# The fifth of seven products: one 512-column matmul for both parts of its operand, and two bank tags exchanged

## The chip, the cores and the metric

The kernel runs on one core of a Trainium2 chip. The metric is the device time of one execution in microseconds. The kernel before took 1758.14 us, the median of three runs (1758.01 to 1759.31).

The engines are named as the profile names them: PE is TensorE (PEld its weight loads), DVE is VectorE, ACT is ScalarE, POOL is GpSimd and SP is SyncE, which issues most transfers. PSUM is the memory that TensorE writes its products to. The program uses it in banks of 128 partitions by 512 float32 values.

## The reference

Two layers of a decoder trunk over 512 tokens of width 1024. In each layer: half a SwiGLU feed-forward, a mixer (a convolution, a sliding-window attention, an attention to a memory), a second half feed-forward, and a norm. Only the feed-forward is touched here:

```python
def swiglu(x, w1, w3, w2):
    return (jax.nn.silu(x @ w1) * (x @ w3)) @ w2

h = x + 0.5 * swiglu(rms_norm(x, ffn1_norm[l]), ffn1_w1[l], ffn1_w3[l], ffn1_w2[l])
...
h = h + 0.5 * swiglu(rms_norm(h, ffn2_norm[l]), ffn2_w1[l], ffn2_w3[l], ffn2_w2[l])
```

The inner width is 2816, that is 22 blocks of 128 columns. All of it is float32.

## The kernel before, in words

**Layout.** Activations are kept transposed: features on the partitions, the 512 tokens along a row. [...] ScalarE makes the high part (line 146) and VectorE subtracts it to get the low one (line 147). `whi` and `wlo` are the parts of a weight, `mh`/`ml` and `xhi`/`xlo` are buffers with the parts of the normed activations (`mh`, in spite of its name, holds high and low parts side by side, as do the three others).

**A feed-forward pass** (four in all) takes the 22 blocks in four quarters of 6, 6, 6 and 4. The first four blocks are done plainly. The other 18 are done in nine pairs, `f` = 4, 6, ... 20, by `up_pair`, and a quarter ends with the blocks' product with `w2` (lines 178 to 180 into the bank `mm`, and the addition to `h` in line 557). The blocks of a quarter's start are made ahead of that, so that pairs and `w2` work lie in each other's neighbourhood.

**A pair** multiplies the 1024 features by 256 columns, for `w1` and for `w3` (`i` = 0 and 1 in the loops), in 512 tokens. Features, columns and tokens are each halved, and the eight products of halves are replaced by seven, in the manner of Strassen and Winograd. Each of the seven has 512 features (4 blocks of 128, `k`), 128 columns and 256 tokens (`QT`). `M.m[j]` is the activations' operand of product number `j`: quarters and sums of quarters, made once in a pass. On the weights' side the sums are made for each pair: `X` is a sum of blocks, made by an ordinary transfer and one that adds (line 368, issued from POOL), in three buffers shared by all pairs, and `raw` gets two more sums by VectorE (line 398).

**Two ways to form a product.** `product` (line 379) uses twelve matmuls of 256 columns and adds all three kinds up in one half of a bank. `beside` (line 387) takes the operand's high and low parts, which lie next to each other, as one operand of 512 columns: four matmuls give high by high in a bank's first half and high by low in its second, and four of 256 columns add low by high to the first half. So it has eight matmuls, and its two halves must then be added, by VectorE.

**Banks.** There are eight: three with the tag `mm`, one `cf`, two `pt` and two `po`. A tag's banks are handed out in turn; a tile that asks for a tag waits until the tile that held that bank before has been read for the last time. The first pair of a pass (`f` = `PLAIN` = 4) uses `product` alone, with banks called `xy` and `zv`. The other eight pairs use banks called `x`, `y`, `c` and `v`. In them, products number 1, 6 and 5 are added up in `x` one after another, and ScalarE copies the sum out after each (lines 424 and 436 and their like); products 2, 3, 7 and 4 use `beside`. There are four passes of eight such pairs with two operands each.

**The order of the work.** The lines of the program say what depends on what. A scheduler in the framework makes one list of instructions for each engine from them, by its own simulated timeline. Each engine then takes its list strictly in order. A change of one product can so move instructions all over the pairs.

Of the kernel before, what the change touches and what calls it, by code (L numbers as in the profile page):

```python
# [13 lines left out]
AF = mybir.ActivationFunctionType  # L14
# [4 lines left out]
P = 128  # L19
D = 1024  # L20
S = 512
# [44 lines left out]
def trunk(ctx: ExitStack, tc: tile.TileContext, xT, memT, pos, w1a, w3a, w2a, w1b, w3b, w2b,  # L66
          wconv, wqk, wvm, wmem, wout, gains, small, rows, consts, out):
    nc = tc.nc
    V, G, A, T = nc.vector, nc.gpsimd, nc.scalar, nc.tensor
# [21 lines left out]
    def bank(shape, tag):  # L91

        if tag == "mm":
            return ps_mm.tile(shape, F32, tag=tag, name=tag)
        return ps_ax.tile(shape, F32, tag=tag, name=tag, bufs=1 if tag == "cf" else 2)

    def tm(name, tag="t", bufs=None):
        return tmp.tile([P, S], F32, tag=tag, name=name, **({"bufs": bufs} if bufs else {}))
# [4 lines left out]
    def raw_tile(src, cols):  # L103
        raw = wst.tile([P, UNIT], F32, tag="raw", name="raw", bufs=3)
        nc.sync.dma_start(raw[:, 0:cols], src)
        return raw
# [5 lines left out]
    first = []  # L112
# [72 lines left out]
    def blk(k, n=P):  # L185
        return slice(k * n, (k + 1) * n)
# [98 lines left out]
    QT = 256  # L285
# [65 lines left out]
    def gated():  # L351
        p = gated_pair()
        return [at(p, ALL, i, ALL) for i in range(2)]

    def unit(x):
        p = pair()
        split(p[0], p[1], x, V)
        return p

    def up_pair(l, w13, f, M):  # L360

        raw = [raw_tile(w13[i][l, f], D) for i in range(2)]
        X = []
        for i in range(2):

            x = wst.tile([P, UNIT], F32, tag="aux", name="wsum", bufs=3)
            nc.sync.dma_start(x.rearrange("p (f c) -> p f c", f=2), w13[i][l, f : f + 2, :, 0:QW].rearrange("f p c -> p f c"))
            G.dma_start(x, w13[i][l, f + 1], accum_op=ALU.add)
            X.append(x)
        z = wst.tile([P, UNIT], F32, tag="raw", name="raw", bufs=3)  # L370
        for i in range(2):
            nc.sync.dma_start(z[:, blk(i, QW)], w13[i][l, f + 1, :, QW:])
        x0, x1 = blk(0, QT), blk(1, QT)

        def product(ps, w, half, j, first=False):


            for n, (part, q) in enumerate([(0, q) for k in range(4) for q in ((k, 0), (k, 1))] + [(1, (k, 0)) for k in range(4)]):
                tail[0] = T.matmul(ps, w[part][:, blk(4 * half + q[0])], M.m[j][q[0]][:, q[1]], skip_group_check=True,  # L379
                                   start=first and not n, stop=n == 11)  # L380

        def beside(ps, w, half, j, first=False):


            def go(out, part, n):
                for k in range(4):
                    tail[0] = T.matmul(out, w[part][:, blk(4 * half + k)], M.m[j][k][:, 0:n], skip_group_check=True,  # L387
                                       start=first and not part and k == 0, stop=part == 1 and k == 3)

            go(ps, 0, 2)  # L390
            go(ps[:, 0], 1, 1)

        u, g = (tmp.tile([P, 2, S], F32, tag=t, name=t, bufs=n) for t, n in (("u", 1), ("g", 2)))
        part = [tm("part", "sq", 2) for _ in range(2)]
        to = (u, g)

        def add(out, a, b):
            V.tensor_tensor(out=out, in0=a, in1=b, op=ALU.add)

        def summed(out, ps, a):  # L400
            add(out, ps[:, 0], a)
            add(out, out, ps[:, 1])

        if f == PLAIN:
            xy = [bank([P, S], "po") for _ in range(2)]
            zv = [bank([P, S], "pt") for _ in range(2)]
            for i in range(2):
                w = unit(raw[i])
                product(xy[i][:, x0], w, 0, 1, first=True)
                product(xy[i][:, x1], w, 1, 2)  # L410
                A.activation(part[i], xy[i], AF.Copy)
                add(to[i][:, 0, x0], part[i][:, x0], part[i][:, x1])

                add(raw[i][:, 0:QW], raw[i][:, 0:QW], X[i][:, QW:])
                add(raw[i][:, QW:], raw[i][:, QW:], raw[i][:, 0:QW])
            for i in range(2):
                w = unit(raw[i])
                product(xy[i][:, x0], w, 0, 6)
                A.activation(part[i][:, x1], xy[i][:, x0], AF.Copy)
                product(zv[i][:, x0], w, 1, 3, first=True)  # L420
            for i in range(2):
                w = unit(X[i])
                product(xy[i][:, x0], w, 1, 5)
                A.activation(part[i][:, x0], xy[i][:, x0], AF.Copy)
                product(zv[i][:, x1], w, 0, 7)
                add(to[i][:, :, x1], zv[i].rearrange("p (n t) -> p n t", n=2), part[i][:, x0].unsqueeze(1).to_broadcast([P, 2, QT]))
            w = unit(z)
            for i in range(2):
                product(zv[i][:, x1], w, i, 4)
                add(to[i][:, 1, x0], zv[i][:, x1], part[i][:, x1])  # L430
        else:
            x = [bank([P, QT], "pt") for _ in range(2)]
            for i in range(2):
                w = unit(raw[i])
                product(x[i], w, 0, 1, first=True)
                A.activation(part[i][:, x0], x[i], AF.Copy)
                y = bank([P, 2, QT], "po")
                beside(y, w, 1, 2, first=True)
                summed(to[i][:, 0, x0], y, part[i][:, x0])

                add(raw[i][:, 0:QW], raw[i][:, 0:QW], X[i][:, QW:])
                add(raw[i][:, QW:], raw[i][:, QW:], raw[i][:, 0:QW])
            c, v = [bank([P, 2, QT], t) for t in ("cf", "mm")], []
            for i in range(2):
                w = unit(raw[i])
                product(x[i], w, 0, 6)
                A.activation(part[i][:, x1], x[i], AF.Copy)
                beside(c[i], w, 1, 3, first=True)
            for i in range(2):
                w = unit(X[i])  # L450
                v.append(bank([P, 2, QT], "po"))
                beside(v[i], w, 0, 7, first=True)
                A.activation(to[i][:, 1, x1], v[i][:, 0], AF.Copy)
                add(to[i][:, 1, x1], to[i][:, 1, x1], v[i][:, 1])
                product(x[i], w, 1, 5)
                A.activation(part[i][:, x0], x[i], AF.Copy)
                summed(to[i][:, 0, x1], c[i], part[i][:, x0])
                add(to[i][:, 1, x1], to[i][:, 1, x1], part[i][:, x0])
            w = unit(z)
            for i in range(2):  # L460
                beside(v[i], w, i, 4)
                summed(to[i][:, 1, x0], v[i], part[i][:, x1])
        out = gated()
        for n, sign in enumerate((1.0, -1.0)):
            A.activation(u[:, n], u[:, n], AF.Silu, scale=sign)
        M.gated = V.tensor_tensor(out=g, in0=g, in1=u, op=ALU.mult)
        for n, sign in enumerate((1.0, -1.0)):
            hi, lo = out[n]
            A.activation(hi, g[:, n], AF.Copy, scale=sign)
            V.scalar_tensor_tensor(out=lo, in0=g[:, n], scalar=sign, in1=hi.bitcast(F32), op0=ALU.mult, op1=ALU.subtract)  # L470
        return out

    def ffn(l, w13, w2, x, sums, factors, last, at_product, aside=None, closing=None):
# [55 lines left out]
        for q, (f0, nf) in enumerate(QUARTERS):  # L529
            ahead = 2 if q + 1 < len(QUARTERS) else 0  # L530
            for f in range(f0, f0 + nf + ahead, 2):
                if f not in g:
                    g[f], g[f + 1] = up_pair(l, w13, f, M)
                    if f == PLAIN:
                        with tc.issue_after(M.gated.ins):
                            rescale = after()
# [615 lines left out]
    for l in range(L):  # L1152
        x, new = nxt.x, Stat("st")
# [163 lines left out]
```

## Time and profile before

| what | us |
|---|---|
| median of three runs | 1758.14 |
| the profiled execution | 1758.82 |
| its span, first to last instruction | 1757.1 |
| TensorE busy | 1738.9 |
| VectorE busy | 1371.8 |
| ScalarE busy | 908.9 |

A row of the profile gives a line of the kernel, an engine, an operation, the tiles it writes and reads (`out<-in`) and their shapes. A busy time counts the time in which at least one instruction of a group ran. Matmuls overlap: a row says 0.39 us for one of 512 columns, while the next one starts after 0.23. For what a group costs, the start of the next group is therefore the measure, and not the sum of durations. An idle time in brackets is what an engine lost before an instruction, with what ended it.

### The profile page before, as it was taken

What the parts mean: (1) busy time and instruction counts of PE and PEld (TensorE: products, weight loads), DVE (VectorE), ACT (ScalarE), POOL (GpSimd) and SP (SyncE); (2) the same over time, 40 slices, a digit from 0 to 9 for tenths busy, and PEclk for the clock granted to TensorE, in tenths of its full rate; (3) what the DMA queues carried; (4) which work ended last, traced back from release to release, by engine and by line L of the source; (5) the groups of instructions that cost most, each with busy time, mean ns of one, the idle gap of its engine ahead of it and who ended that gap; (6) DMA issues with size and microseconds to landing.
All of it is one profiled execution on the core that took longest, in us unless ns stands there. A gap on an engine that the chain in (4) does not pass through costs nothing.

```text
span 1757.1 us, 26371 instructions
## 1 busy us (share of the span) xinstructions
PE 1738.9 (99%) x9980; PEld 1521.3 (87%) x9980; DVE 1371.8 (78%) x2218; ACT 908.9 (52%) x1437; POOL 196.5 (11%) x220
## 2 busy tenths in 40 slices
PE   8999999999999999999999999999999999999998
PEld 6889889888888989898889898988888889898987
DVE  6969878689877868687778787776898768686866
ACT  5546445356765535353655364544567655353533
POOL 1001000006221000000010010000251210000000
PEclk9999999999999999999999999999999999999999
DMA  9456645256348546465565565552661666464632
GB/s 272 121 173 162 174 132 156 78 159 155 96 87 190 131 136 171 139 166 146 146 155 158 154 169 156 156 144 68 167 160 57 136 152 177 132 174 128 156 99 85
DMA packets 97199, 253.49 MB, mean 144 GB/s; under 512 B 9904, under 2 KB 16304, under 8 KB 97072
## 3 DMA queue, kind: packets, MB, share of 16 engines
q1 hardware_dynamic: 78064, 190.45, 34.5%
q0 software_dynamic: 19008, 61.35, 19.4%
q8 instruction: 79, 1.29, 0.3%
q14 instruction: 48, 0.39, 0.1%
HBM read 249.67 MB, written 2.10 MB: 143 GB/s over the span
## 4 chain that ended last, share of the span: by engine, by line
PE 95%; DVE 2%; DMA 1%; issue 1%; ACT 0%; SPq 0%; DVEq 0%; POOLq 0%; ACTq 0%
PE pt L379 16%; PE mm L178 14%; PE mm L180 14%; PE mm L179 14%; PE po L387 14%; PE cf L387 2%; PE mm L387 2%; PE po L379 2%; PE po L178 2%; PE po L180 2%; PE po L179 2%; PE po L921 2%; PE mm L869 1%; DMA wsum<-in_w3a 1%; PE cf L178 1%; PE cf L179 1%
## 5 line engine op out<-in xcount | busy, mean ns | idle before, releaser
L146 ACT ACTIVATE whi<-raw 128x1024 fp32r<-128x1024 f32 (+3 forms) x346 | 326.1, 947 | 445.4 <-PE mm L179 218.6
L147 DVE TENSOR_TENSOR wlo<-raw,whi 128x1024 fp32r<-128x1024 f32 (+3 forms) x346 | 375.7, 1089 | 98.6 <-ACT whi L146 94.1
L179 PE MATMUL mm<-glo,whi 128*128 128x512 f32 (+1 forms) x752 | 292.2, 389 | 0.0
L178 PE MATMUL mm<-ghi,whi 128*128 128x512 f32 (+1 forms) x752 | 291.8, 390 | 0.0
L180 PE MATMUL mm<-ghi,wlo 128*128 128x512 f32 (+1 forms) x734 | 285.2, 389 | 0.0
L557 DVE SCALAR_TENSOR_TENSOR h<-mm,h 128x512 f32<-128x512 f32 x126 | 86.4, 689 | 117.2 <-PE mm L180 116.9
L178 PEld LDWEIGHTS mm<-ghi,whi 128*128 128x128 f32 x752 | 141.3, 188 | 29.2 <-DVE h L557 1.2
L179 PEld LDWEIGHTS mm<-glo,whi 128*128 128x128 f32 x752 | 141.3, 188 | 28.0
L180 PEld LDWEIGHTS mm<-ghi,wlo 128*128 128x128 f32 x734 | 137.9, 188 | 27.8
L387 PE MATMUL po<-xlo,whi 128*128 128x512 f32 x512 | 139.2, 393 | 0.0
L1051 DVE SCALAR_TENSOR_TENSOR there<-ypad,par,there 128x512 f32<-128x512 f32 x180 | 136.0, 779 | 1.5 <-issue 0.2
L178 PE MATMUL mm<-xhi,whi 128*128 128x512 f32 x272 | 108.6, 403 | 6.3 <-ACT xhi L156 6.3
L180 PE MATMUL mm<-xhi,wlo 128*128 128x512 f32 x272 | 107.1, 394 | 0.0
L179 PE MATMUL mm<-xlo,whi 128*128 128x512 f32 x272 | 107.0, 393 | 0.0
L387 PEld LDWEIGHTS po<-xlo,whi 128*128 128x128 f32 x512 | 89.6, 189 | 13.5
L147 DVE TENSOR_TENSOR wlo<-wsum,whi 128x1024 fp32r<-128x1024 f32 x72 | 87.6, 1217 | 0.6 <-ACT whi L146 0.4
L387 PEld LDWEIGHTS po<-xlo,wlo 128*128 128x128 f32 x512 | 78.3, 188 | 10.6
L146 ACT ACTIVATE whi<-wsum 128x1024 fp32r<-128x1024 f32 x72 | 76.2, 1059 | 20.3 <-PE po L387 16.4
L379 PE MATMUL pt<-xhi,whi 128*128 128x256 f32 x576 | 81.8, 283 | 0.0
L387 PE MATMUL po<-xlo,wlo 128*128 128x256 f32 x512 | 81.2, 280 | 0.0
L379 PEld LDWEIGHTS pt<-xhi,whi 128*128 128x128 f32 x576 | 74.9, 190 | 0.6
L379 PE MATMUL pt<-ml,whi 128*128 128x256 f32 x512 | 72.9, 282 | 0.0
(389 smaller groups left out, 3583.0 us busy)
## 6 DMA issues: line engine op xcount, KB each, us to landing
raw<-in_w2a SPq DMA_DIRECT2D x48, 384.0 KB, 3.5
raw<-in_w2b SPq DMA_DIRECT2D x48, 384.0 KB, 3.6
raw<-in_w1b SPq DMA_DIRECT2D x26, 512.0 KB, 3.5
raw<-in_w3b SPq DMA_DIRECT2D x26, 512.0 KB, 3.6
raw<-in_w1a SPq DMA_DIRECT2D x25, 512.0 KB, 3.5
raw<-in_w3a SPq DMA_DIRECT2D x25, 512.0 KB, 3.7
wsum<-in_w1a SPq DMA_DIRECT2D x18, 512.0 KB, 4.5
wsum<-in_w3a SPq DMA_DIRECT2D x18, 512.0 KB, 3.6
```

The lines of the kernel that those rows point to most:

```text
L146: a = A.activation(hi, x, AF.Copy)
L147: return a, on.tensor_tensor(out=lo, in0=x, in1=hi.bitcast(F32), op=ALU.subtract)
L178: T.matmul(ps, a[0], b[0], start=first, stop=False, **more)
L179: T.matmul(ps, a[0], b[1], start=False, stop=False, **more)
L180: tail[0] = T.matmul(ps, a[1], b[0], start=False, stop=last, **more)
L379: tail[0] = T.matmul(ps, w[part][:, blk(4 * half + q[0])], M.m[j][q[0]][:, q[1]], skip_group_check=True, start=first and not n, stop=n == 11)
L387: tail[0] = T.matmul(out, w[part][:, blk(4 * half + k)], M.m[j][k][:, 0:n], skip_group_check=True, start=first and not part and k == 0, st ...
L557: added = V.scalar_tensor_tensor(out=h[:, d, :], in0=ps, scalar=0.5, in1=h[:, d, :], op0=ALU.mult, op1=ALU.add)
L869: tail[0] = T.matmul(pp[i][:, z, :], q, k, start=not masked, stop=True, skip_group_check=True)
L921: tail[0] = T.matmul(po[:, 2 * c + i, :], ptb[:, i, j, :], v, start=(j == 0), stop=(j == nk - 1))
L1051: V.scalar_tensor_tensor(out=cv[:, c, :], in0=ypad[:, c, j : j + S], scalar=conv_w[:, c, j : j + 1], in1=cv[:, c, :], op0=ALU.mult, op1=AL ...
```

## The change

In the eight pairs after the first of each pass, product number 5 is formed with `beside` instead of `product`. Its bank `x` now has two halves. Products 1 and 6 use the first half alone, as before. Product 5 writes its high-by-low part to the second half, which nothing has written since the bank was begun, so it starts from nothing there. After ScalarE's copy of the first half into `part`, VectorE adds the second half to it.

In the first pair of each pass the tags of `xy` and `zv` are exchanged: `xy` takes `pt` and `zv` takes `po`. So the `x` of the next pair (tag `pt`) now follows on `xy`, and its `y` (tag `po`) on `zv`; before, it was the other way round.

```diff
         if f == PLAIN:
-            xy = [bank([P, S], "po") for _ in range(2)]
-            zv = [bank([P, S], "pt") for _ in range(2)]
+            xy = [bank([P, S], "pt") for _ in range(2)]
+            zv = [bank([P, S], "po") for _ in range(2)]
...
         else:
-            x = [bank([P, QT], "pt") for _ in range(2)]
+            x = [bank([P, 2, QT], "pt") for _ in range(2)]
             for i in range(2):
                 w = unit(raw[i])
-                product(x[i], w, 0, 1, first=True)
-                A.activation(part[i][:, x0], x[i], AF.Copy)
+                product(x[i][:, 0], w, 0, 1, first=True)
+                A.activation(part[i][:, x0], x[i][:, 0], AF.Copy)
                 y = bank([P, 2, QT], "po")
                 beside(y, w, 1, 2, first=True)
...
-                product(x[i], w, 0, 6)
-                A.activation(part[i][:, x1], x[i], AF.Copy)
+                product(x[i][:, 0], w, 0, 6)
+                A.activation(part[i][:, x1], x[i][:, 0], AF.Copy)
                 beside(c[i], w, 1, 3, first=True)
...
-                product(x[i], w, 1, 5)
-                A.activation(part[i][:, x0], x[i], AF.Copy)
+                beside(x[i], w, 1, 5)
+                A.activation(part[i][:, x0], x[i][:, 0], AF.Copy)
+                add(part[i][:, x0], part[i][:, x0], x[i][:, 1])
                 summed(to[i][:, 0, x1], c[i], part[i][:, x0])
                 add(to[i][:, 1, x1], to[i][:, 1, x1], part[i][:, x0])
```

The instruction lists of the two kernels, at three places. In the changed kernel, lines after 455 have a number one higher. First, TensorE in the first pass, at the end of pair `f` = 6: the fifth product of both operands (`pt`), product 4 or 7 (`po`) and the first matmuls of the product with `w2` (`mm`). Before:

```order
L379 MATMUL pt<-xhi,whi 128x256 x8
L379 MATMUL pt<-xhi,wlo 128x256 x4
L387 MATMUL po<-xlo,whi 128x512 x4
L387 MATMUL po<-xlo,wlo 128x256 x4
L178 MATMUL mm<-ghi,whi 128x512
L179 MATMUL mm<-glo,whi 128x512
L379 MATMUL pt<-xhi,whi 128x256 x8
```

And now:

```order
L387 MATMUL pt<-xhi,whi 128x512 x4
L387 MATMUL pt<-xhi,wlo 128x256 x4
L178 MATMUL mm<-ghi,whi 128x512
L179 MATMUL mm<-glo,whi 128x512
L387 MATMUL po<-xlo,whi 128x512 x4
L387 MATMUL po<-xlo,wlo 128x256 x4
L387 MATMUL pt<-xhi,whi 128x512 x4
```

The twelve matmuls of a fifth product have become eight, and two `w2` matmuls have moved ahead of the `po` product.

Second, TensorE in the first pass where the first pair (lines 379 alone) passes into pair `f` = 6, from the first operand's last `xy` product on. Before:

```order
L379 MATMUL po<-xhi,whi 128x256 x8
L379 MATMUL po<-xhi,wlo 128x256 x4
L379 MATMUL pt<-xlo,whi 128x256 x2
L387 MATMUL po<-mh,whi 128x512 x2
L387 MATMUL po<-ml,whi 128x512 x2
L379 MATMUL po<-xhi,whi 128x256 x8
L379 MATMUL po<-xhi,wlo 128x256 x4
L379 MATMUL pt<-xlo,whi 128x256 x7
```

And now:

```order
L379 MATMUL pt<-xhi,whi 128x256 x8
L379 MATMUL pt<-xhi,wlo 128x256 x4
L379 MATMUL po<-xlo,whi 128x256 x2
L379 MATMUL pt<-mh,whi 128x256 x8
L379 MATMUL pt<-xhi,whi 128x256 x8
L379 MATMUL pt<-xhi,wlo 128x256 x4
L379 MATMUL po<-xlo,whi 128x256 x7
```

The first work of pair 6 used to be its `y` (`po<-mh`, line 387) and is now its `x` (`pt<-mh`, line 379). Either way it follows the same two matmuls.

Third, VectorE in the first pass, near the end of pair `f` = 8, up to a split of the next weights (`wlo<-raw,whi`); `ypad` is a table that is made meanwhile. Before:

```order
L398 TENSOR_TENSOR u<-u,po 128x256
L601 TENSOR_TENSOR ypad<-ypad 128x128
L398 TENSOR_TENSOR u<-cf,part 128x256
L398 TENSOR_TENSOR g<-g,po 128x256
L698 TENSOR_TENSOR ypad<-ypad,gmem 128x256
L599 TENSOR_SCALAR ypad<-ypad 128x128
L398 TENSOR_TENSOR u<-u,cf 128x256
L580 SCALAR_TENSOR_TENSOR ypad<-ypad 128x128
L601 TENSOR_TENSOR ypad<-ypad 128x128
L147 TENSOR_TENSOR wlo<-raw,whi 128x1024
```

And now:

```order
L398 TENSOR_TENSOR u<-u,po 128x256
L602 TENSOR_TENSOR ypad<-ypad 128x128
L398 TENSOR_TENSOR part<-part,pt 128x256
L398 TENSOR_TENSOR g<-g,po 128x256
L699 TENSOR_TENSOR ypad<-ypad,gmem 128x256
L398 TENSOR_TENSOR part<-part,pt 128x256
L600 TENSOR_SCALAR ypad<-ypad 128x128
L398 TENSOR_TENSOR u<-cf,part 128x256
L581 SCALAR_TENSOR_TENSOR ypad<-ypad 128x128
L398 TENSOR_TENSOR u<-u,cf 128x256
L602 TENSOR_TENSOR ypad<-ypad 128x128
L147 TENSOR_TENSOR wlo<-raw,whi 128x1024
```

The two new additions (`part<-part,pt`) stand ahead of the split. The lists of the mixer, outside the feed-forward passes, are the same in both kernels, but for numbers.

## The prediction

> **What bounds the kernel now.** I read the page's first and fourth parts, then TensorE's waits, then its timeline in a calm stretch, then VectorE's share stage by stage. The busy line and the chain that ended last:
>
> ```profile
> PE 1738.9 (99%) x9980; PEld 1521.3 (87%) x9980; DVE 1371.8 (78%) x2218; ACT 908.9 (52%) x1437; POOL 196.5 (11%) x220
> PE 95%; DVE 2%; DMA 1%; issue 1%; ACT 0%; SPq 0%; DVEq 0%; POOLq 0%; ACTq 0%
> ```
>
> TensorE is the bound: 99% busy, 95% of the chain. A microsecond taken off its stream is a microsecond off the span, unless another engine cannot follow. The view of waits, TensorE alone, says how much idleness is left to win:
>
> ```profile
> PE mm L178 <- ACT xhi L156: 6.3, 2, 6.1
> ...
> PE po L387 <- ACT part L424: 0.7, 1, 0.7
> PE cf L387 <- ACT whi L146: 0.7, 2, 0.5
> PE po L387 <- DVE wlo L147: 0.6, 1, 0.6
> PE po L387 <- DVE u L398: 0.5, 1, 0.5
> PE pt L379 <- DVE g L398: 0.4, 1, 0.4
> ```
>
> The 6.3 us is the start of the program. The other five rows, 2.9 us together, all belong to the first two or three pairs of a feed-forward pass, and they are all that better order could give back there.
>
> **The change: TensorE's part.** Before and after, a fifth product streams 12 x 256 = 3072 columns; `beside` streams 4 x 512 + 4 x 256, also 3072. So no arithmetic is saved, only four instructions out of twelve. What four instructions are worth is read from TensorE's timeline of a pair in which it never waits; the columns are start, duration, operation and count, and the start of the next group ends the one before:
>
> ```profile
> 241.82 1.11 PE L379 MATMUL pt<-ml,whi 128*128 128x256 f32 x8
> ...
> 243.25 1.09 PE L387 MATMUL cf<-xhi,whi 128*128 128x512 f32 x4
> ...
> 244.65 1.11 PE L379 MATMUL pt<-ml,whi 128*128 128x256 f32 x8
> ...
> 246.08 1.09 PE L387 MATMUL mm<-xhi,whi 128*128 128x512 f32 x4
> ...
> 247.49 1.09 PE L387 MATMUL po<-xlo,whi 128*128 128x512 f32 x4
> ```
>
> A product of twelve takes 243.25 - 241.82 = 1.43 us, and 246.08 - 244.65 = 1.43 again; one of eight takes 244.65 - 243.25 = 1.40 and 247.49 - 246.08 = 1.41. The gain is 0.02 to 0.03 us each; I take 0.03 and, since the rows are rounded, allow 0.02 to 0.04. How many there are is the count of the ScalarE copies that follow a fifth product:
>
> ```profile
> L456 ACT ACTIVATE part<-pt 128x256 f32<-128x256 f32 x64 | 24.0, 375 | 14.2 <-PE pt L379 13.4 <-ACT u L453 0.8
> ```
>
> 64 x 0.03 = 1.9 us saved (bounds 1.3 and 2.6).
>
> [...]
>
> **VectorE's part.** Each of the 64 products now leaves its two parts in two halves of a bank, so VectorE gains 64 additions of 128x256, one operand from a bank. Its nearest rows are the other additions of line 398 that take 256 columns; the group and two neighbours in the timeline:
>
> ```profile
> L398 DVE TENSOR_TENSOR g<-g,part 128x256 f32<-128x256 f32 x32 | 13.3, 417 | 0.2
> ```
>
> ```profile
> 163.55 0.42 DVE L398 TENSOR_TENSOR g<-g,part 128x256 f32<-128x256 f32 x1
> 163.88 0.41 DVE L398 TENSOR_TENSOR g<-g,mm 128x256 f32<-128x256 f32 x1
> ```
>
> One lasts 0.42 us and the next starts after 0.33, so each new addition takes 0.33 us of the queue: 64 x 0.33 = 21 us of VectorE work, two (0.67 us) to a pair. ScalarE's copy of the first half stays as it was. Whether it counts depends on the stretch. By stage, the columns being length, then busy time and count of PE, PEld, DVE, ACT, POOL:
>
> ```profile
> 55.00:93.00 38.00, 36.68 (x276) 34.63 (x276) 36.73 (x51) 24.67 (x37) 3.02 (x4) 1.00 0.59 148
> 140.00:200.00 60.00, 59.32 (x401) 54.46 (x401) 58.31 (x125) 36.12 (x63) 8.62 (x8) 1.00 0.64 162
> 328.00:360.00 32.00, 32.00 (x190) 28.22 (x190) 20.91 (x36) 16.42 (x29) 0.11 (x1) 1.00 0.24 66
> 924.00:965.00 41.00, 40.45 (x306) 38.49 (x305) 35.65 (x50) 24.51 (x36) 3.46 (x4) 1.00 0.60 158
> 1012.00:1062.00 50.00, 49.53 (x343) 45.89 (x342) 45.05 (x77) 31.46 (x50) 5.95 (x6) 1.00 0.66 174
> 1446.00:1480.00 34.00, 34.00 (x266) 33.09 (x265) 32.15 (x43) 22.57 (x33) 2.59 (x3) 1.00 0.54 149
> ```
>
> In 328 to 360, a lone pair, VectorE is idle for 11 of 32 us; there 0.67 us is covered by that idleness (and would cost up to 0.67 us a pair without it). In the other five VectorE is 87 to 97% busy. The same windows, for the copies of line 456 alone, count the fifth products in them:
>
> ```profile
> 55.00:93.00 38.00, 0.39 (x1) 1.00 0.59 148
> 140.00:200.00 60.00, 1.95 (x6) 1.00 0.64 162
> 924.00:965.00 41.00, 0.37 (x1) 1.00 0.60 158
> 1012.00:1062.00 50.00, 1.52 (x4) 1.00 0.66 174
> 1446.00:1480.00 34.00, 0.37 (x1) 1.00 0.54 149
> ```
>
> Thirteen additions fall where VectorE is crowded: 13 x 0.33 = 4.3 us if every one reaches TensorE, nothing if none does. Most of that I do not charge, because TensorE hardly waits there as it is: 0.68 us in 140 to 200, and 0.47 in 1012 to 1062. What is behind the new addition in VectorE's queue matters at one point, the split of a pair's summed weights, whose end frees the buffer for the next sum's transfers. From the chain of waits and VectorE's timeline:
>
> ```profile
> 169.17 0.10 DVE wlo L147
> ...
> 170.43 4.52 DMA wsum<-in_w3a
> ...
> 175.50 6.52 DMA wsum<-in_w3a
> ...
> 184.69 1.20 PE cf L387 x4
> ```
>
> ```profile
> 157.26 1.23 DVE L147 TENSOR_TENSOR wlo<-raw,whi 128x1024 fp32r<-128x1024 f32 x1 [0.67 <-ACT whi L146]
> ```
>
> ```profile
> 1034.11 0.42 DVE L398 TENSOR_TENSOR g<-po,part 128x256 f32<-128x256 f32 x1 [1.42 <-PE po L387]
> ```
>
> Two transfers, one behind the other, lead from that split to the wait at 184.69. If the split is later, so is everything after it. In the changed order the two additions of the pair stand ahead of the split that started at 157.26, where VectorE sat idle for 0.67 us: the wait takes them up, exactly and with nothing over. One more small table instruction of 0.2 us has come ahead of the split of 169.17. So this chain costs 0.2 us if the cover holds and 0.9 if it does not. At its twin in the second layer the idle 1.42 us at 1034 covers 0.67 with room: 0, or 0.67 without cover. I charge 0.5 us for both, between 0.2 and 1.6.
>
> **The banks.** Before, the next pair's `y` waits for the first pair's `xy`, and its `x` for `zv`; now it is the other way round. TensorE's two waits at that crossing in the first pass:
>
> ```profile
> 69.94 0.74 PE L387 MATMUL po<-mh,whi 128*128 128x512 f32 x2 [0.71 <-ACT part L424]
> ```
>
> ```profile
> 77.33 0.50 PE L387 MATMUL po<-mh,wlo 128*128 128x256 f32 x2 [0.57 <-DVE wlo L147]
> ```
>
> The first is a wait for ScalarE's last copy out of `xy`. Whatever takes that bank next waits for the same copy; now it is the 256-column product instead. The second is for the low part of the second weight, which the new order asks for at the same place. VectorE's list is the same up to there. So the swap moves no wait: 0, between -1.3 us (both vanish) and +1.4 (0.67 us of the new additions at each of two crossings).
>
> **Sum.** -1.9 + 0.5 + 0 = -1.4 us. The profiled execution took 1758.82 us for a span of 1757.1; against that, 1757.4. The median of the three runs is 1758.14, 0.68 below it, and the forecast for a median is 1758.14 - 1.4 = 1756.7 us.
>
> **The rivals.** *VectorE becomes the bound in the crowded stretches.* For it: 97% busy in two of them, and every addition sits ahead of a split that TensorE needs. Against it: outside those stretches a third of its time is free, and the scheduler has put additions into known waits. All thirteen give +4.3 - 1.9 = +2.4: 1760.5, slower than before. It is slower by over 0.2% (3.5 us; that is about what a measurement of this kernel tells from no change) once 5.4 us of waiting appear, which is 16 additions, so three from calmer stretches besides. Chance 0.2, and for over 0.2% 0.14.
>
> *The swap works.* The first pair's early bank now serves the product that opens the next pair, and the waits at the crossings go. For it: all 2.9 us of the rows above stand in these early pairs. Against it: their releasers are copies and splits, whose place in the order has not changed. All of it gives -1.9 - 2.9 = -4.8: 1753.3; half of it, 1754.8, is not yet 0.2%. Chance 0.16.
>
> *The change does not save what it seems to.* The 0.03 us is the difference of two rounded starts. If a `beside` in the `x` bank is no shorter than a product, 0 + 0.5 gives 1758.6. [...] For it: equal columns; against it: each of the two pairs of rows shows a difference. Chance 0.12.
>
> **How the numbers follow.** The forecast keeps 0.52, with a range of its own from 1755.4 to 1758.1. Over 0.2% faster is below 1754.6: most of the second rival and a tail of the forecast, 0.17. Slower is above 1761.7: 0.14 from the first rival and 0.01 from anything else, 0.15. Within 0.2%: 0.68. The range reaches half a microsecond past the second rival's 0.2% point, and to the first rival's full price: 1753.6 to 1760.5, with about a tenth left out on each side.
>
> **What would show it.** Right: the fifth product's group appears as 8 matmuls of line 387 into `pt`, with 1.40 us to the next group; 64 new additions of about 0.42 us on VectorE; TensorE's waits, without the start's, still near 3 us. Wrong: `wlo` splits that start later against the matmuls before them, new waits of TensorE for `DVE wlo` or `DVE part` in 140 to 200 or 1012 to 1062, more than 1.6 us together (the first rival), or the waits for `part` and `wlo` at 70 and 77 gone (the second). A group of 1.43 us after the change would mean the third. A difference outside the pairs would upset the whole reading, since the mixer's order is as it was.

## The result, and the profile after

The changed kernel takes 1775.89 us (median of five runs, 1773.15 to 1778.9), the kernel before 1758.42 beside it (five runs, 1758.01 to 1759.31). The ratio is 1.0097, with a 95% interval from 1.0086 to 1.0109: slower by 17 us, where 1756.7 was forecast. The profiled execution took 1778.20 us for a span of 1776.4.

The busy line and the chain that ended last, from the page of the changed kernel:

```profile
PE 1743.8 (98%) x9724; PEld 1510.0 (85%) x9724; DVE 1389.5 (78%) x2282; ACT 906.7 (51%) x1437; POOL 196.2 (11%) x220
PE 86%; DVE 5%; DMA 4%; issue 2%; ACT 1%; SPq 0%; DVEq 0%; ACTq 0%; POOLq 0%
```

TensorE's share of the chain falls from 95 to 86%; VectorE and transfers take it. The span grew by 19.3 us. Span less busy time, TensorE's idleness, was 18.2 us and is 32.6, so 14.4 of them are waits; the other 4.9 are longer busy time, in spite of 256 matmuls fewer. The view of TensorE's waits (total, times, longest) names the waits:

```profile
PE po L387 <- DVE g L398: 11.1, 8, 2.3
PE mm L178 <- ACT xhi L156: 6.1, 1, 6.1
PE mm L387 <- ACT whi L146: 2.1, 5, 1.0
PE cf L387 <- ACT whi L146: 2.1, 5, 0.4
```

The first row is new: eight times a `beside` into `po` waits for the addition that empties its bank (for product 4, the addition that reads product 7's second half out of the bank, before product 4 may be added up there), near 178, 278, 698, 793, 1086, 1156, 1575 and 1670 us, two in each feed-forward pass. The third row is new too, and the fourth was 0.7; the matmuls of these follow on the stalls. They are not all of one kind. At 178 (1.35 us) VectorE is simply crowded, as these rows of its timeline show; the addition that empties the bank comes behind a split and table instructions:

```profile
176.80 1.21 DVE L147 TENSOR_TENSOR wlo<-raw,whi 128x1024 fp32r<-128x1024 f32 x1
177.94 0.88 DVE L659 SCALAR_TENSOR_TENSOR sg<-sn,rw 128x128 f32<-128x128 f32 x4
178.74 0.28 DVE L581 SCALAR_TENSOR_TENSOR ypad<-ypad 128x128 f32<-128x128 f32 x1
178.95 0.41 DVE L398 TENSOR_TENSOR g<-g,po 128x256 f32<-128x256 f32 x1
```

At 1086 (0.34 us) the addition stands behind a split for which VectorE sits idle for 5.00 us, until ScalarE has made the high part. The other six, 9.4 of the 11.1 us, are where the second of three pairs done in a row passes into the third (from `f` = 16 to 18 in all four passes, from 10 to 12 in two), and there VectorE idles too. The prediction had opened none of these six.

**One of the six.** VectorE's timeline at the end of the third quarter (a duration behind the start; in brackets the idle time before). The kernel before:

```profile
264.03 1.22 DVE L147 TENSOR_TENSOR wlo<-wsum,whi 128x1024 fp32r<-128x1024 f32 x1
265.50 1.22 DVE L147 TENSOR_TENSOR wlo<-wsum,whi 128x1024 fp32r<-128x1024 f32 x1
...
269.72 0.69 DVE L398 TENSOR_TENSOR raw<-raw,wsum 128x512 f32<-128x512 f32 x1
...
272.76 0.68 DVE L398 TENSOR_TENSOR raw<-raw 128x512 f32<-128x512 f32 x1
...
273.69 0.41 DVE L398 TENSOR_TENSOR g<-g,po 128x256 f32<-128x256 f32 x1
275.73 0.69 DVE L398 TENSOR_TENSOR raw<-raw,wsum 128x512 f32<-128x512 f32 x1 [1.62 <-DMA wsum<-in_w3a]
```

And the changed kernel:

```profile
265.17 0.42 DVE L398 TENSOR_TENSOR u<-po,part 128x256 f32<-128x256 f32 x1 [2.27 <-PE po L387]
265.52 1.21 DVE L147 TENSOR_TENSOR wlo<-wsum,whi 128x1024 fp32r<-128x1024 f32 x1
...
268.52 1.22 DVE L147 TENSOR_TENSOR wlo<-wsum,whi 128x1024 fp32r<-128x1024 f32 x1
...
274.99 0.41 DVE L398 TENSOR_TENSOR part<-part,pt 128x256 f32<-128x256 f32 x1
279.95 0.69 DVE L398 TENSOR_TENSOR raw<-raw,wsum 128x512 f32<-128x512 f32 x1 [4.56 <-issue]
280.56 0.41 DVE L398 TENSOR_TENSOR g<-g,po 128x256 f32<-128x256 f32 x1
...
281.23 0.68 DVE L398 TENSOR_TENSOR raw<-raw 128x512 f32<-128x512 f32 x1
```

The second `raw<-raw,wsum` is the new pair's sum for its second operand; it must wait until `X` has landed. (The row of the changed kernel names no releaser, only `issue`; but the adding transfer, issued at 270.91, takes 9.0 us, which makes 279.9.) Before, it came behind everything that others needed: behind `raw<-raw`, the second sum of the first operand, and behind `g<-g,po`, which empties the bank for product 4. Now both stand behind it, and VectorE takes its list in order. TensorE and ScalarE, from the changed kernel's timeline:

```profile
278.06 0.64 PE L379 MATMUL pt<-mh,wlo 128*128 128x256 f32 x4
281.03 1.58 PE L387 MATMUL po<-xlo,whi 128*128 128x512 f32 x4 [2.34 <-DVE g L398]
```

```profile
282.00 1.06 ACT L146 ACTIVATE whi<-raw 128x1024 fp32r<-128x1024 f32 x1 [7.16 <-DVE raw L398]
```

TensorE loses 2.34 us for the bank, and the next weights are split late as well.

**Why the transfer is late.** TensorE itself is 1.35 us later at that place: the same group `mm<-xhi,wlo`, the end of product 3, starts at 266.82 before and at 268.17 now. This group serves as the yardstick from here on, since the runs differ by some us in where they stand. Against it, the first `wlo<-wsum` split is on time (1.49 us later) and the second 1.7 us late (3.02 later): two splits of `glo` and one more addition have come between them. It is 1.7 us late at all six places. SP's queue of transfers waits for that split: it ends at 266.72 before and at 269.74 now, and the first issue below comes 0.02 us after either end. The issues, before and after:

```profile
266.74 0.38 SPq L367 DMA_DIRECT2D wsum<-in_w1a  x1
267.88 0.34 SPq L372 DMA_DIRECT2D raw<-in_w1a  x1
268.27 0.42 SPq L372 DMA_DIRECT2D raw<-in_w3a  x1
```

```profile
269.76 0.38 SPq L367 DMA_DIRECT2D wsum<-in_w1a  x1
270.90 0.34 SPq L372 DMA_DIRECT2D raw<-in_w1a  x1
271.29 0.42 SPq L372 DMA_DIRECT2D raw<-in_w3a  x1
```

The adding transfer on which the sum waits is `wsum<-in_w3a`, issued on POOL at 270.32 before and 270.91 now. The median from issue to landing, of the one transfer in this stretch, is the last column, before and after:

```profile
wsum<-in_w3a POOLq DMA_DIRECT2D x1, 512.0 KB, 5.4
```

```profile
wsum<-in_w3a POOLq DMA_DIRECT2D x1, 512.0 KB, 9.0
```

The stretches ahead of and in that transfer (the last two columns are the busy share of the transfer engines and GB/s), before and after:

```profile
266.70:270.30 3.60, 3.60 (x29) 3.42 (x28) 3.54 (x6) 2.05 (x4) 0.00 (x0) 1.00 0.71 246
270.30:275.70 5.40, 5.40 (x41) 5.06 (x40) 3.26 (x7) 3.01 (x6) 1.73 (x2) 1.00 1.04 245
```

```profile
267.00:270.90 3.90, 3.90 (x28) 3.58 (x27) 3.90 (x7) 2.65 (x5) 0.00 (x0) 1.00 0.45 141
270.90:275.00 4.10, 4.10 (x29) 3.71 (x28) 4.10 (x8) 2.10 (x4) 1.72 (x2) 1.00 0.85 217
275.00:280.00 5.00, 3.69 (x28) 3.31 (x26) 0.44 (x3) 0.00 (x0) 0.00 (x0) 1.00 1.03 215
```

So the late split left the transfer engines half idle (a busy share of 0.45, 141 GB/s) until 270.9, and then the three loads behind it ran together with the adding transfer. That the overlap is what makes it 9.0 us long is read from these rows; no run held it apart by itself.

**The clock.** Twice, right behind the waits of 2.34 and 1.83 us, the granted clock (third column from the end) is half for 3.41 us. The first of the two, from the changed kernel's windows:

```profile
281.60:285.00 3.40, 3.40 (x12) 2.80 (x11) 3.40 (x8) 2.80 (x4) 0.00 (x0) 0.51 0.00 0
```

Half of 3.41 us, twice, is 3.4 us of the longer busy time, as an estimate. In the first stretch four matmuls of 512 columns into `cf` take 1.73 us to the next group (283.26 to 284.99), where they take 0.92 in the kernel before (278.64 to 279.56). About as much again (4.9 + 1.9 saved - 3.4 = 3.4) I have not assigned; groups of matmuls just behind a wait look longer in the rows (at 700.05, 1157.61 and 1576.30 four into `po` take 1.03 to 1.04 us to the next group, where those at 275.70 take 0.93).

### The profile page after: what moved, and what is told of

It reads as the page before. It is cut to its first block, busy times and chain, and to the rows that moved or that the text cites. A ratio compares the mean times of both kernels' runs of the same rounds, so it can differ in the third digit from the quotient of the medians.

```text
span 1776.4 us, 25902 instructions
## 1 busy us (share of the span) xinstructions
PE 1743.8 (98%) x9724; PEld 1510.0 (85%) x9724; DVE 1389.5 (78%) x2282; ACT 906.7 (51%) x1437; POOL 196.2 (11%) x220
## 4 chain that ended last, share of the span: by engine, by line
PE 86%; DVE 5%; DMA 4%; issue 2%; ACT 1%; SPq 0%; DVEq 0%; ACTq 0%; POOLq 0%
PE mm L178 13%; PE mm L180 13%; PE mm L179 13%; PE po L387 12%; PE pt L379 11%; PE pt L387 4%; PE mm L387 2%; PE cf L387 2%; PE po L379 2%; PE po L922 2%; PE po L178 1%; PE po L180 1%; PE po L179 1%; DMA wsum<-in_w3b 1%; DVE wlo L147 1%
## 5 line engine op out<-in xcount | busy, mean ns | idle before, releaser
L387 PE MATMUL po<-xlo,whi 128*128 128x512 f32 x512 | 140.4, 396 | 11.1 <-DVE g L398 11.1
L379 PE MATMUL pt<-mh,whi 128*128 128x256 f32 x608 | 85.8, 283 | 0.7 <-ACT part L424 0.7
L379 PE MATMUL pt<-ml,whi 128*128 128x256 f32 x608 | 85.6, 282 | 0.3 <-ACT part L436 0.3
L379 PEld LDWEIGHTS pt<-ml,whi 128*128 128x128 f32 x608 | 79.5, 190 | 2.4 <-ACT part L436 0.5
```

## The experiments

Theories at the start: the **swap** of banks; VectorE's **load**, 64 additions of 0.33 us; and the **list**, VectorE's new order together with the late transfer.

**The swap alone, and the product alone.** The first takes only this from the change:

```diff
-            xy = [bank([P, S], "po") for _ in range(2)]
-            zv = [bank([P, S], "pt") for _ in range(2)]
+            xy = [bank([P, S], "pt") for _ in range(2)]
+            zv = [bank([P, S], "po") for _ in range(2)]
```

> The kernel before with the exchanged bank tags alone; the fifth product keeps its twelve matmuls and there is no new addition. Theory Q (queue: in the changed kernel's VectorE list the sum that waits for the second operand's adding transfer stands ahead of the addition that frees a po bank and of the first operand's second sum, so both are late by the transfer's lateness): VectorE's list of the middle pair of a quarter is here as in the kernel before, so 1757 to 1760 us and no wait of TensorE for that addition above 0.5 us. Rival S (the swap makes the waits): 1772 to 1778. Rival L (the 64 new additions load VectorE): 1757 to 1760, as under Q.

The second takes all the rest (its main lines):

```diff
-                product(x[i], w, 1, 5)
-                A.activation(part[i][:, x0], x[i], AF.Copy)
+                beside(x[i], w, 1, 5)
+                A.activation(part[i][:, x0], x[i][:, 0], AF.Copy)
+                add(part[i][:, x0], part[i][:, x0], x[i][:, 1])
```

> The changed kernel with the old bank tags: the fifth product in eight matmuls and its addition, no swap. Theory Q: the middle pair's list is the changed kernel's, with the waiting sum ahead of the freeing addition, so 1771 to 1779 us with six or more waits of TensorE of 1 to 2.5 us at the same place. Rival S: 1755 to 1758. Rival L: 1773 to 1779.

Measured: the swap 1757.85 us, ratio 0.9991 (0.9982 to 1.0000); the product 1776.54, ratio 1.0101 (1.0086 to 1.0116). All of the loss is the product's, and the swap costs nothing. In the trace of the second the sum stands ahead of the bank's addition as in the whole change:

```profile
277.32 0.69 DVE L398 TENSOR_TENSOR raw<-raw,wsum 128x512 f32<-128x512 f32 x1 [4.67 <-issue]
277.93 0.41 DVE L398 TENSOR_TENSOR g<-g,po 128x256 f32<-128x256 f32 x1
```

**Order against load.** The changed kernel, with a rule for the scheduler: the second operand's waiting sum goes behind the addition that empties the second operand's `po` bank, and behind the first operand's second sum. Additions and transfers stay as many. (Not shown: `before_sum` begins as an empty list, and `add` returns its instruction.)

```diff
-                add(raw[i][:, 0:QW], raw[i][:, 0:QW], X[i][:, QW:])
-                add(raw[i][:, QW:], raw[i][:, QW:], raw[i][:, 0:QW])
+                with ExitStack() as behind:
+                    for o in M.before_sum if i else ():
+                        behind.enter_context(tc.issue_after(o.ins))
+                    add(raw[i][:, 0:QW], raw[i][:, 0:QW], X[i][:, QW:])
+                    M.before_sum.append(add(raw[i][:, QW:], raw[i][:, QW:], raw[i][:, 0:QW]))
...
-                add(to[i][:, 1, x1], to[i][:, 1, x1], v[i][:, 1])
+                M.before_sum = [add(to[i][:, 1, x1], to[i][:, 1, x1], v[i][:, 1])]
```

> The changed kernel, all its work kept, with one rule of order on VectorE: the second operand's sum with a transferred block is issued behind the pair before's addition that frees the second po bank, and behind the first operand's second sum. Theory Q: TensorE's 11 us of waits for that addition go; the transfer is as late as before, so a part comes back as a wait for ScalarE's high part of the second operand's sum: 1757 to 1764 us. Rival L (load): the same 64 additions, so 1772 to 1779.

Measured: 1763.48 us, ratio 1.0028 (1.0017 to 1.0039). The order gives back 12 of the 17 us with all 64 additions in place. The transfers are still late: at the six places the waiting sum starts 10.3 to 12.1 us behind `mm<-xhi,wlo`, where it is 8.6 to 9.8 in the kernel before and 10.2 to 11.8 in the changed one.

**The load by itself.** The kernel before, with 64 additions of the same shape whose result nobody uses:

```diff
                 A.activation(part[i][:, x0], x[i], AF.Copy)
+                add(tm("junk", "pr", 1)[:, x0], part[i][:, x0], x[i])
```

> The kernel before with its twelve matmuls for product 5 and no swap, and 64 additions of 128x256 more on VectorE, each reading the x bank and the copy and writing a buffer that nobody uses. The list of VectorE comes out new: in the middle pair of a quarter the split of the second X is late, as in the changed kernel, and the po-freeing addition stands behind the second waiting sum, but the first operand's second sum stands ahead of it. Theory Q (late transfer and queue, called forth by the additions): 1762 to 1776. If the shorter fifth product upsets the order: 1757 to 1760.

Measured: 1771.68 us, ratio 1.0076 (1.0062 to 1.0089). By the time alone this looks like the load; its trace says otherwise. VectorE in the same stretch:

```profile
273.82 0.69 DVE L398 TENSOR_TENSOR raw<-raw,wsum 128x512 f32<-128x512 f32 x1 [2.09 <-issue]
...
274.76 0.41 DVE L398 TENSOR_TENSOR g<-g,po 128x256 f32<-128x256 f32 x1
```

The idle additions have made the scheduler put `g<-g,po` behind the waiting sum (the first operand's `raw<-raw` stays ahead of it), and TensorE's waits are the same row, 8.2 us in six. Here the sum is not late: at the six places it starts 8.8 to 9.5 us behind `mm<-xhi,wlo`, much as in the kernel before. But TensorE's list is new too. It asks for the bank 9.1 us behind that group, where the changed kernel asks after 10.5. So this run does not separate load from list; it shows that additions which nobody waits for are enough to call such a list forth.

**The splits first.** The changed kernel, with the `X` splits preferred by the scheduler, meant to free the buffers and send the loads out earlier:

```diff
-                w = unit(X[i])
+                with tc.high_priority():
+                    w = unit(X[i])
```

> The changed kernel with a higher scheduling priority for the splits of the summed weights X, all its work kept. The list of VectorE comes out otherwise: in the middle pair of a quarter the first operand's second sum and the freeing addition now stand ahead of the second waiting sum, while the splits of X are no earlier. In another pair of the first passes the freeing addition now stands behind that sum. Theory Q: most of the waits go, 1757 to 1767 us. Rival L: the same load, 1772 to 1779. If the late splits alone decide (theory T, the transfers' lateness whatever the list): 1770 to 1779.

Measured: 1759.88 us, ratio 1.0011 (1.0001 to 1.0021): 16 of the 17 us. But this list differs in its order too: at all six places `g<-g,po` and the first operand's `raw<-raw` stand ahead of the waiting sum again. VectorE in the same stretch:

```profile
272.95 0.41 DVE L398 TENSOR_TENSOR g<-g,po 128x256 f32<-128x256 f32 x1
...
275.50 0.69 DVE L398 TENSOR_TENSOR raw<-raw,wsum 128x512 f32<-128x512 f32 x1 [1.80 <-issue]
```

Against TensorE the second split is only 0.3 us earlier than in the changed kernel, the adding transfer takes 8.5 us, and the sum starts 11.0 us behind `mm<-xhi,wlo`. So here too it is the order that was put right; what an early transfer is worth, this run does not show.

**Both aids.**

> The changed kernel with both aids: the rule of order on VectorE of the first ordered kernel, and the higher priority for the splits of X. All work kept. Theory Q: no wait of TensorE for the po-freeing addition; the gain of the shorter product (about 2 us) can show: 1755 to 1760 us. Rival L (load of the 64 additions): 1772 or more; already at odds with the two runs above.

Measured: 1762.37 us, ratio 1.0026 (1.0015 to 1.0036). Together they are not clearly better than the rule alone (1763.48) and worse than the splits first (1759.88); each change of a rule makes a new list with waits of its own (here `cf` for `wlo`, 3.0 us in four). That the two gains would add up was wrong.

**A wider rule.** As the rule above, but the waiting sum goes behind every addition of the pair before that empties a `po`, `mm` or `cf` bank, for both operands:

```diff
+                if not i:
+                    M.before_sum = []
+                M.before_sum.append(add(to[i][:, 1, x1], to[i][:, 1, x1], v[i][:, 1]))
...
-                summed(to[i][:, 0, x1], c[i], part[i][:, x0])
+                M.before_sum.append(summed(to[i][:, 0, x1], c[i], part[i][:, x0]))
```

> The changed kernel with a wider rule: the second operand's waiting sum goes behind every addition of the pair before that frees the banks po, cf and mm as far as product 5 feeds them, and behind the first operand's second sum. Theory Q, with the waits for cf of the narrower rule (2.5 us) gone too: 1755 to 1760 us. If a sum that is issued so late makes the second operand's high part late: 1760 to 1766, with waits for ACT whi.

Measured: 1753.80 us, ratio 0.9971 (0.9961 to 0.9982): faster than both kernels, with all the additions of the change. Its profile:

```profile
PE 1735.8 (99%) x9724; PEld 1507.2 (86%) x9724; DVE 1391.1 (79%) x2282; ACT 911.1 (52%) x1437; POOL 196.3 (11%) x220
```

VectorE is as busy as in the changed kernel (1389.5 us), and TensorE's waits for `DVE g` are 0.4 us. VectorE's load does not set the time.

**The order alone.** The kernel before, without any addition, with the bad order put in by hand at the six places (`f` = 18 in each pass, `f` = 12 in two):

```diff
-                add(raw[i][:, 0:QW], raw[i][:, 0:QW], X[i][:, QW:])
-                add(raw[i][:, QW:], raw[i][:, QW:], raw[i][:, 0:QW])
+                waiting = add(raw[i][:, 0:QW], raw[i][:, 0:QW], X[i][:, QW:])
+                if i and (f == 18 or f == 12 and w13[0] is w1b):
+                    put_behind(M.frees, waiting)
+                    put_behind(second, waiting)
+                second = add(raw[i][:, QW:], raw[i][:, QW:], raw[i][:, 0:QW])
...
-                add(to[i][:, 1, x1], to[i][:, 1, x1], v[i][:, 1])
+                M.frees = add(to[i][:, 1, x1], to[i][:, 1, x1], v[i][:, 1])
```

> The kernel before, all its work, with the bad order put in by hand: at the last pair of the third quarter of each pass, and at that of the second quarter in the second and fourth, the freeing addition and the first operand's second sum go behind the second waiting sum. The splits of X, and so the transfers, stay as early as they were (landed at 275.7 us where the changed kernel has 280). If the order alone decides: six places at 1.5 to 2.5 us, 1768 to 1775. If it takes the order and the later transfers together (theory Q as the traces have it): TensorE asks for the bank at 277.1 and has it by 276.8, so at most 0.5 us a place, 1758 to 1761.

Measured: 1764.79 us, ratio 1.0037 (1.0024 to 1.0049), between what the theories said. The splits are as early against TensorE as in the kernel before, and at this place the sum starts 10.0 us behind `mm<-xhi,wlo` (265.86), against 8.9 before and 11.8 in the changed kernel:

```profile
275.88 0.69 DVE L398 TENSOR_TENSOR raw<-raw,wsum 128x512 f32<-128x512 f32 x1 [3.67 <-DMA wsum<-in_w3a]
276.49 0.41 DVE L398 TENSOR_TENSOR g<-g,po 128x256 f32<-128x256 f32 x1
```

Measured from that group, the addition that empties the bank starts 3.8 us later than in the kernel before, and 1.8 earlier than in the changed one. The order alone costs 6 us, a third of the loss.

The six places side by side show how order and lateness work together. With this order TensorE asks for the bank 10.5 us behind the group, in the changed kernel and in this one, and 1.1 us pass from the sum's start to the product's (279.95 to 281.03). So every start of the sum later than 9.4 us should become a wait of TensorE. The sum's start behind the group, and TensorE's wait for `DVE g`, in us:

| place in the changed kernel | sum, before | sum, changed | wait, changed | sum, by hand | wait, by hand |
|---|---|---|---|---|---|
| 278 | 8.9 | 11.8 | 2.34 | 10.0 | 0.64 |
| 698 | 9.0 | 11.1 | 1.67 | 9.2 | none |
| 793 | 8.6 | 11.3 | 1.83 | 9.0 | none |
| 1156 | 9.8 | 11.0 | 1.55 | 8.3 | none |
| 1575 | 9.5 | 10.7 | 1.25 | 10.4 | 0.99 |
| 1670 | 9.8 | 10.2 | 0.75 | 10.2 | 0.82 |

All twelve waits come out to within 0.1 us.

**The transfer alone.** The changed kernel without the adding transfer of the second operand, so that a part of the arithmetic is left out, and as a control the kernel before without it:

```diff
-            G.dma_start(x, w13[i][l, f + 1], accum_op=ALU.add)
+            if not i:
+                G.dma_start(x, w13[i][l, f + 1], accum_op=ALU.add)
```

> The changed kernel without the transfer that adds the other block to the second operand's X (the first operand's stays), so the second operand's X is computed from one block only: that part of the arithmetic is left out. VectorE's list in the middle pairs stays exactly that of the changed kernel: the sum that reads X still stands ahead of g<-g,po and of the first operand's second sum, but its X now lands about 4 to 7 us earlier (one transfer of the chain less). If the 17 us need both, the order and the late transfer behind it, the sum no longer waits and the time is 1756 to 1761. If the order of the list decides alone, 1764 or more, as in the kernel before with that order by hand. If the load of 64 additions decides, 1772 or more.

> The kernel before without the same adding transfer (the second operand's X is computed from one block only: that part of the arithmetic is left out). It is the control for the changed kernel without it: the waits that this transfer causes in the kernel before are under 1 us, so 1756.5 to 1758.5 if its absence is worth nothing of its own and the changed kernel's gain without it comes from its list no longer waiting. If the absence of 64 transfers is itself worth much, 1745 or less, and then that experiment does not tell.

Measured: 1754.74 us, ratio 0.9975 (0.9966 to 0.9985), and for the control 1756.32, ratio 0.9989 (0.9979 to 0.9998). In this stretch VectorE's list of the first is that of the changed kernel:

```profile
271.34 0.68 DVE L399 TENSOR_TENSOR raw<-raw,wsum 128x512 f32<-128x512 f32 x1
271.94 0.41 DVE L399 TENSOR_TENSOR g<-g,po 128x256 f32<-128x256 f32 x1
```

The sum does not wait, what stands behind it does not either, and the loss is gone: where `X` is there in time the order costs nothing. The transfer's absence is worth 2 us by itself, by the control.

**What the product's new form is worth.** The kernel with the wider rule once more, and the same with the old fifth product, on one chip:

```diff
-                beside(x[i], w, 1, 5)
+                product(x[i][:, 0], w, 1, 5)
                 A.activation(part[i][:, x0], x[i][:, 0], AF.Copy)
-                add(part[i][:, x0], part[i][:, x0], x[i][:, 1])
```

> The kernel with the wide rule of order on VectorE and the swapped banks, but with the fifth product in twelve matmuls and without the new addition: what the form of the product itself is worth once the order does not get in the way. By the term of the prediction (64 x 0.03 us) it is 1.9 us above the kernel with the rule, near 1755.7; if the product saves nothing, or its addition costs what it saves, the two are equal, near 1753.8; if the rule alone is what gains, this one is below it.

> The kernel with the wide rule once more, beside the one without the product's new form on the same chip: 1752.5 to 1755.

Measured: 1756.36 us without the new form, ratio 0.9986 (0.9976 to 0.9995), and 1753.96 with it, ratio 0.9972 (0.9962 to 0.9982). The difference is 2.4 us. Each ratio's interval is taken against the kernel before, and these overlap; the twelve and eleven times of the two kernels, resampled directly against each other, give a 95% interval from 1.0 to 3.9 us. The pair without the adding transfer, which was timed on two chips, says nearly the same (1756.32 against 1754.74, 1.6 us).

## Why the prediction was wrong

**TensorE's term held.** A fifth product takes 1.40 us to the next group (268.65 to 270.05 in the changed kernel's timeline) where it took 1.43. The 1.9 us are there in both pairs of kernels that differ in this and have no such stall: 2.4 and 1.6 us. TensorE's busy time is less by 1.7 us in the first pair (1737.0 against 1735.3) and by 2.1 in the second (1737.6 against 1735.5). So the rival that the change saves nothing falls; the lists of the two kernels of a pair differ too, and no run holds the product alone apart from them.

**The banks held.** Zero was charged, and the swap alone has a ratio of 0.9991 (0.9982 to 1.0000).

**The additions' own price held.** There are 64 of 0.41 us, and the kernel with the wider rule carries them all and is 5 us faster than the one before. The first rival, VectorE as the bound in crowded stretches, named the right sign, and the stall at 178 is of its kind: 1.35 us, in the stretch from 140 to 200 that it named. The other 9.7 us stand behind 3 to 5 us in which VectorE *idles*. Its price per addition, and its point of 16 additions, have nothing to do with those.

**The step that failed is the + 0.5.** There the prediction said that what is behind the new addition matters "at one point", the split of the summed weights, and took from one pair's list that this and its twin in the second layer would cost 0.2 to 1.6 us together. Three things were wrong in it.

- The place. I compared VectorE's list in one pair of the first pass (`f` = 8) and took it for all. The list changes most at the six places, which I did not open. There the second split is 1.7 us late against TensorE, not 0.2 to 0.9.
- The amplification. I let a late split delay the next transfers by as much. At the place shown, 1.7 us of split have become 9.0 instead of 5.4 us for the adding transfer that the loads now overlap, and the sum is 2.9 us later against TensorE. At the other five it is 0.4 to 2.7 us later.
- The order. I asked how long instructions take and not what stands behind one that waits. The scheduler moved no work of weight; it put a sum that waits for a transfer ahead of two instructions that TensorE and ScalarE wait for. By itself that costs 6 us (order by hand) or nothing (transfer in time); with the late transfer it is most of the 17.

So the loss of the changed kernel needs both. With the order put right and the sum still late, 5 us (the first rule) or 2 us (the splits first) are left of it; with the order alone, by hand, 6; with the transfer left out and the order as it was, nothing. The idle additions show another way to the same wait: the sum no later, but TensorE asking for the bank earlier. The two aids do not add up, and a better list than either rule's may exist. Why the scheduler's own timeline holds the waiting sum for the earlier one was not examined.

**What would have shown it.** The two lists were there to be compared for every pair. In VectorE's list at each of the six places the second `raw<-raw,wsum` stands ahead of `g<-g,po` and of `raw<-raw`, where it stood behind; and the profile of before has the price tag: the sum at 275.73 waited 1.62 us for a transfer, with nothing behind it that was wanted. An instruction that already waits for a transfer is the one to watch.

## What to carry to other kernels

When the order is made by a scheduler, an added instruction costs what the new list costs, not its own duration: compare the lists at every place where an instruction waits for a transfer, and ask what now stands behind it on its engine. If such a sum, split or copy has come ahead of an addition that empties a bank, put it behind by a rule; here that turned a loss of 17 us into a gain of 5, about half of which is the new product's and half the new list's. An experiment that adds idle work to measure "load" moves the list as well, so read its trace before its time.

## What the runs showed of the hardware

**VectorE took its list in order.** In the changed kernel three instructions that needed nothing from the transfer (starts at 280.56, 280.89 and 281.23) stood behind one that did, for which VectorE had idled 4.56 us.

**Behind two waits of the changed kernel the granted clock was half.** I had not expected it. The two stretches, 3.41 us each, start 0.62 us after the end of the wait of 2.34 us and 1.45 us after that of 1.83. From 12 us on, until TensorE's last work, the trace's record of the clock has no other, so none behind a wait of 1.67 us or less. The two start 515.41 us apart, 151.0 times 3.413. By the estimate above each costs 1.7 us, so here the two waits cost 4.0 and 3.5 us.

For the other kernels I go by the mean granted clock; one such stretch, 1.7 us of the span, takes 0.001 off it. In the profiled executions it was 0.998 in the kernel before and 0.996 in the changed one, 0.996 with the product alone (longest wait after the program's start 2.4 us), 0.997 with the idle additions (1.7 us) and 0.998 with the splits first (1.8 us). As an estimate, that is two stretches with the product alone, one with the idle additions and none with the splits first. In two of the changed kernel's other four executions the mean was 0.998. So these runs give no length of wait from which the clock falls, and what makes it fall was not shown.
